# One side stream with larger loads in a hybrid attention layer: modulation and weight sums share two tiles, stores move to ScalarE's queue, biases are scaled later

## The chip, the cores and the metric

The kernel runs on one core of a Trainium2 chip. A core has a matrix engine (TensorE, PE in the profile; PEld is its loading of weights), VectorE (DVE), ScalarE (ACT), GpSimd (POOL) and SyncE (SP), which here does nothing but issue transfers. Each engine works through its own instructions in order. A transfer (DMA) is issued by an engine and then carried out by sixteen DMA engines; the issuing engine goes on. Where an instruction must wait for another engine or for a transfer, everything behind it on its engine waits as well. The metric is the device time of one execution in microseconds (us), lower is better.

## What is computed

One layer of a streaming encoder on 1024 frames of width 1024, in float32. Two attention branches of eight heads each work on the same normalised, modulated input; a gated convolutional feed-forward part follows. Cut to what matters:

```python
mod = silu(c) @ w_ada + b_ada
sh1, sc1, g1, sh2, sc2, g2 = split(mod, 6)
h = layer_norm(x) * (1 + sc1) + sh1
proj = h @ w_in          # q, k, v, forget of branch A; q, k, v of branch C; two gates
o_a = forgetting_attention(q_a, k_a, v_a, f_a + b_f)     # causal, bias from forget gates
o_c = chunk_band_attention(q_c, k_c, v_c, rel_bias)      # 64-frame chunks, 8 chunks back
merged = sigmoid(gate_a) * (o_a @ w_br_fox) + sigmoid(gate_c) * (o_c @ w_br_chunk)
x = layer_norm(alpha * x + (1 + g1) * (merged @ w_out), ln1_g, ln1_b)
h = layer_norm(x) * (1 + sc2) + sh2
a, val = split(causal_conv(h @ w_up), 2)
x = layer_norm(alpha * x + (1 + g2) * ((silu(a) * val) @ w_down), ln2_g, ln2_b)
```

## The kernel before, in words

**Products in two halves.** A float32 operand is parted into a rounded half and a remainder, and a product is made of three matmuls. For weights the rounding is a copy on ACT (L104) and the remainder a subtraction on POOL (L105, tile `wl`).

**Order of the work.** The kernel is written as one long list of operations. A planner in the compiler then gives each engine its order: it keeps to the order of the source as a priority, but an operation whose inputs and tiles are free may be taken earlier than operations of other engines that stand ahead of it in the source. A tile named with `tag` and `bufs` takes turns in that many buffers; a load into a buffer waits for the last reader of what was there.

**Attention.** Sixteen heads in eight pairs, four pairs of the chunked branch first (4, 5, 6, 7), then four of the forgetting branch (2, 3, 0, 1). For each head there are four steps of two query tiles. `scores` makes the logits on PE, adds the bias on DVE (L464) and takes the exponential on ACT (L470). `probs` turns the result on PE (L504), and ACT (L507) and DVE (L508) part it into halves in `pt`. `weighted` multiplies with the values (L518), and ACT and DVE add the two halves of the output into `o32` (L522, L523). Between the steps the loop takes units from `stream`: the projections to q, k, v and to the gates, which are the other half of PE's work in this stage. Each call of `stream.step()` yields about 2.6 us of matmuls by the source's own costs, and the loop takes as many as keep pace with attention.

**Biases.** `prep` is called for a head well before its turn. It moves the halves of the keys (L407, L408) and loads the bias. For the chunked branch that is a 128x640 table (`cb`, L414), which DVE scales at once (L415) and in which POOL fills two corners (L416, L417). For the forgetting branch it is a spread row of sums (`fb`, L411), to which POOL adds the causal mask (`fm`, L430) for each query tile.

**Stores.** A gate unit ends with a tanh on ACT (L395) into `sg`, and an output pair ends with L523. Both append their store, issued by SP, to a list `stores`, and `begun()` issues what is in the list at the next call of the stream (L295). `inverted` writes the inverse row sums through `rt` (L479, L480).

**Two side streams.** Two generators run beside, each advanced by one `yield` with every call of the stream; what is left is run behind the loop (L746).

- `late_modulation` makes the four modulation vectors that attention doesn't need. There are 64 pieces of `w_ada` (four vectors, two halves of 512 columns, eight row blocks). Each is loaded by itself (`wa`, 256 KB, two buffers, L535), multiplied by a column of `cond` on ACT (L546 for the first, L548), and added into `acc` on POOL (L549). After eight pieces PE sums `acc` over the partitions (L167), and DVE adds the bias vector (L161, L163).
- `up_sums` and `down_sums` make sums and differences of weight quarters for the feed-forward part, which multiplies by a scheme with seven products in place of eight. Nineteen times, `four` loads two weight blocks of 512 KB into one tile `dr` with a single buffer (L563), makes four sums on POOL (L568), and stores 1 MB to a scratch tensor, `wd` or `td` (L571).

Of the kernel before, what the change touches and what calls it, by code (L numbers as in the profile page):

```python
# [43 lines left out]
def body(ctx, tc, a, out):  # L44
# [337 lines left out]
    def unit_g():  # L382
        gi = next(gates)

        def run(ws):
            wh, wl = ws[0]
            for half in range(2):
# [8 lines left out]
                stores.append(partial(sy.dma_start, out=gd[half, gi], in_=sg))  # L396
# [4 lines left out]
    def prep(ip, i):  # L401
# [10 lines left out]
        else:  # L412
            b = ap.tile([P, 640], F32, name=nm("cb"), tag="bias")
            sy.dma_start(out=b, in_=a["rel_t"][h])  # L414
            ve.tensor_scalar_mul(b, b, 1.0 / SCALE)  # L415
            po.memset(b[0:DH, 576:640], NEG)  # L416
            po.memset(b[DH:P, 0:64], NEG)  # L417
        return q[i], m1, m2, b, br, h
# [6 lines left out]
    def masked(n, i):  # L425

        (ip, hi, g), qi = steps[n], 2 * steps[n][2] + i
        if ip < 4 and (n, i) not in masks:
            fm = ap.tile([P, P], F32, name=nm("fm"), tag="fm", bufs=5)
            po.tensor_tensor(out=fm, in0=heads[ip, hi][3][:, qi * P : (qi + 1) * P], in1=cmask, op=ALU.add)  # L430
            masks[n, i] = fm
# [41 lines left out]
    def inverted(ip):  # L473
# [4 lines left out]
        rt = ap.tile([n, P], F32, name=nm("rt"), tag="rt", bufs=1)  # L478
# [46 lines left out]
    def late_modulation():  # L525


        pieces = [(v, half, k) for v in (2, 4, 3, 5) for half in range(2) for k in range(KD)]
        ws = {}

        def load(n):
            if n < len(pieces):
                v, half, k = pieces[n]
                ws[n] = ap.tile([P, 1, H], F32, name=nm("wa"), tag="wa", bufs=2)
                sy.dma_start(out=ws[n], in_=ada_src(v, half * H, H)[:, k : k + 1, :])  # L535
# [5 lines left out]
        yield  # L541
        for n, (v, half, k) in enumerate(pieces):
            w = ws.pop(n)[:, 0, :]
            if k == 0:
                acc = ap.tile([P, H], F32, name=nm("acc"), tag="acc", bufs=1)
                se.mul(out=acc, in_=w, mul=cond[:, 0:1])  # L546
            else:
                se.mul(out=w, in_=w, mul=cond[:, k : k + 1])  # L548
                po.tensor_tensor(out=acc, in0=acc, in1=w, op=ALU.add)  # L549
            yield  # L550
            load(n + 2)
            if k == KD - 1:
                ps = pmm.tile([P, H], F32, name=nm("psada"), tag="mm")
                ada_sums(ps, acc, H)
                yield
                ada_bias(ps, v, half * H, H, v != 3)
            yield

    def four(steps, srcs, dst):

        x = ap.tile([P, 4, H], F32, name=nm("dr"), tag="dr", bufs=1)
        for r in range(2):
            sy.dma_start(out=x[:, 2 * r : 2 * r + 2, :], in_=srcs[r])  # L563
        yield
        yield
        yield
# [830 lines left out]
```

## Time and profile before

| | us |
|---|---|
| median of 3 runs | 1657.08 (1655.88 to 1660.12) |
| the profiled execution | 1653.7 |
| its span, first to last instruction | 1651.8 |
| PE busy | 1535.3 |
| DVE busy | 1032.1 |
| ACT busy | 789.8 |
| POOL busy | 597.1 |

The granted clock of PE is 0.970 of full speed over the span. Attention with its side streams lies at about 112 to 765 us. In a row of the timeline the numbers are the start, the duration, the engine and line, and in brackets how long the engine stood idle before it and what ended that. In a row of waits they are the total, the number of times and the longest wait. A name on the left of an arrow is written, names on the right are read; L12 is line 12 of the kernel before. SPq, ACTq and the like are an engine's queue of issues.

### The profile page before, as it was taken

How to read it: one execution, taken by the hardware profiler on the slowest of the kernel's cores; microseconds unless marked ns; L12 is line 12 of the kernel's file. 1: busy time of each engine (PE TensorE's matmuls, PEld its weight loads, DVE VectorE, ACT ScalarE, POOL GpSimd, SP SyncE). 2: the span in 40 equal slices, each digit the busy share in tenths (PEclk: the TensorE clock that was granted, in tenths of full speed). 3: DMA queues.
4: the chain of work that ended last, by engine and by line, in shares of the span. 5: the costliest groups of instructions: out<-in, count | busy, mean ns of one | idle time of the engine just before them, and what ended most of it. 6: DMA issues, size and time to landing. Idle time of an engine off the chain costs nothing. (4 is left out here: it accounts for less than half of the span.)

```text
span 1651.8 us, 22170 instructions
## 1 busy us (share of the span) xinstructions
PE 1535.3 (93%) x7693; PEld 1286.5 (78%) x7693; DVE 1032.1 (62%) x2053; ACT 789.8 (48%) x1420; POOL 597.1 (36%) x455
## 2 busy tenths in 40 slices
PE   6899889969899999998799796999999999999996
PEld 3788778859788988887677685788888888888885
DVE  6746444435444545454759978577777766856788
ACT  3447445444555555453223536444544554456451
POOL 1125536554652342223205365554455455100000
PEclk9999989979999999999999898999999999999998
DMA  9037656666643334324754624543353222597552
GB/s 363 27 103 228 206 186 209 202 207 212 213 152 99 98 122 127 109 103 150 245 180 153 237 111 158 191 140 122 129 177 135 102 96 85 198 385 239 186 196 75
DMA packets 119535, 274.82 MB, mean 166 GB/s; under 512 B 11776, under 2 KB 20672, under 8 KB 119424
## 3 DMA queue, kind: packets, MB, share of 16 engines
q1 hardware_dynamic: 114144, 264.42, 47.5%
q10 hardware_dynamic: 4752, 7.17, 1.2%
q0 software_dynamic: 528, 1.84, 0.3%
q8 instruction: 60, 0.98, 0.2%
q14 instruction: 51, 0.42, 0.1%
HBM read 197.51 MB, written 67.47 MB: 160 GB/s over the span
## 5 line engine op out<-in xcount | busy, mean ns | idle before, releaser
L105 POOL TENSOR_TENSOR wl<-ws,wh 128x1024 fp32r<-128x1024 f32 x54 | 133.4, 2474 | 263.3 <-ACT wh L104 260.6
L826 PE MATMUL psu<-hc,wx 128*128 128x512 f32 x720 | 168.4, 389 | 0.0
L826 PEld LDWEIGHTS psu<-hc,wx 128*128 128x128 f32 x720 | 135.2, 188 | 28.0
L1062 DVE SCALAR_TENSOR_TENSOR pcv<-u,convp,pcv 128x1024 f32<-128x1024 f32 x88 | 113.1, 1285 | 45.3 <-ACT pcv L1060 44.4
L568 POOL TENSOR_TENSOR dr<-dr 128x512 f32<-128x512 f32 x76 | 98.2, 1292 | 79.4 <-DMA dr<-in_w_down 48.1
L1203 DVE TENSOR_TENSOR op<-rw,op 128x512 fp32r<-128x512 f32 x146 | 93.6, 687 | 52.6 <-ACT op L1202 52.1
L1202 ACT CAST op<-rw 128x512 fp32r<-128x512 f32 x146 | 85.3, 623 | 83.4 <-PE psd L1215 39.5
L1214 PE MATMUL psd<-op,op 128*128 128x512 f32 x292 | 113.7, 389 | 0.9 <-DVE op L1203 0.9
L508 DVE TENSOR_TENSOR pt<-pst,pt 128x512 fp32r<-128x512 f32 (+1 forms) x192 | 97.1, 520 | 27.8 <-ACT pt L507 26.1
L1213 PE MATMUL psd<-op,op 128*128 128x512 f32 x292 | 113.6, 389 | 0.0
L1215 PE MATMUL psd<-op,op 128*128 128x512 f32 x292 | 113.6, 389 | 0.0
L470 ACT ACTIVATE s<-s,mx 128x640 f32<-128x640 f32 (+7 forms) x128 | 94.4, 737 | 37.9 <-DVE mx L464 35.9
L507 ACT CAST pt<-pst 128x512 fp32r<-128x512 f32 (+1 forms) x192 | 82.2, 451 | 59.9 <-PE pst L504 57.7
L207 PE MATMUL psg<-h1h,wh 128*128 128x512 f32 x256 | 105.6, 412 | 0.0
L207 PE MATMUL psq<-h1h,wh 128*128 128x512 f32 x256 | 104.4, 409 | 0.4 <-DVE h1h L203 0.4
L209 PE MATMUL psq<-h1h,wl 128*128 128x512 f32 x256 | 101.1, 395 | 2.7 <-POOL wl L105 2.7
L518 PE MATMUL pso<-pt,vs 128*128 128x256 f32 x608 | 93.8, 292 | 10.0 <-ACT pt L507 7.0
L208 PE MATMUL psq<-h1l,wh 128*128 128x512 f32 x256 | 101.4, 396 | 1.7 <-DVE h1l L204 1.7
L504 PE MATMUL pst<-ident,s 128*128 128x128 f32 x528 | 83.6, 278 | 20.5 <-DVE pt L508 20.4
L209 PE MATMUL psg<-h1h,wl 128*128 128x512 f32 x256 | 100.8, 394 | 0.0
L208 PE MATMUL psg<-h1l,wh 128*128 128x512 f32 x256 | 100.6, 393 | 0.0
L518 PEld LDWEIGHTS pso<-pt,vs 128*128 128x128 f32 x608 | 83.7, 194 | 19.4 <-ACT pt L507 11.2
(261 smaller groups left out, 3934.9 us busy)
## 6 DMA issues: line engine op xcount, KB each, us to landing
ws<-in_w_up SPq DMA_DIRECT2D x36, 512.0 KB, 3.7
wa<-in_w_ada SPq DMA_DIRECT2D x64, 256.0 KB, 3.9
dr<-in_w_down SPq DMA_DIRECT2D x22, 512.0 KB, 4.5
td<-dr SPq DMA_DIRECT2D x11, 1024.0 KB, 4.5
rw<-td SPq DMA_DIRECT2D x44, 256.0 KB, 4.5
yd<-y SPq DMA_DIRECT2D x20, 512.0 KB, 2.8
rw<-yd SPq DMA_DIRECT2D x40, 256.0 KB, 3.9
rw<-sd SPq DMA_DIRECT2D x33, 256.0 KB, 4.6
```

The source lines that it names most:

```text
L105: po.tensor_sub(out=lo, in0=st, in1=hi)
L207: pe.matmul(ps, wh, xh, start=start, stop=False)
L208: pe.matmul(ps, wh, xl, start=False, stop=False)
L209: pe.matmul(ps, wl, xh, start=False, stop=stop)
L508: ve.tensor_sub(out=dl, in0=src, in1=dh)
L518: pe.matmul(ps[:, 0:256], vs[:, h % 2, j0 + j, :], pt[j // 4][:, c, j % 4, :], start=j == 0 and c == 0, stop=j == nj - 1 and c == 1)
L568: po.tensor_tensor(out=x[:, o, :], in0=x[:, p, :], in1=x[:, q, :], op=op)
L826: pe.matmul(ps, w[:, a_, k, :], h[k][b_], start=first, stop=k == 3 and a_ == 1, skip_group_check=on)
L1062: ve.scalar_tensor_tensor(out=ps, in0=u[b][:, 2 - d : S + 2 - d], scalar=cp[:, 2 - d : 3 - d], in1=ps, op0=ALU.mult, op1=ALU.add)
L1213: pe.matmul(ps[t], g[:, 0, ts], d[:, 0], start=start, stop=False, skip_group_check=on)
L1214: pe.matmul(ps[t], g[:, 0, ts], d[:, 1], start=False, stop=False, skip_group_check=on)
L1215: pe.matmul(ps[t], g[:, 1, ts], d[:, 0], start=False, stop=stop, skip_group_check=on)
```

## The change

The two side streams become one, `side_work`. Its list of 35 groups has a weight-sum group and a modulation group by turns, and three weight-sum groups at the end. All groups use one tile `dr` of 128x4x512 with two buffers. A modulation group is four row blocks, loaded with one transfer of 1 MB; a weight-sum group has two loads of 512 KB as before. The load for group n + 2 is issued at the end of group n. Within a group two multiplies (and their adds), or two sums, stand between one `yield` and the next. The partition sums of a finished half vector stay in `ps`, and the DVE operation that adds the bias vector (`due`) is issued at the beginning of the next weight-sum group.

The stores of gate tiles are issued by ACT right behind the tanh, and those of outputs are still appended to `stores` but issued by ACT. The scaling of `cb` and the two fills leave `prep`: the tile is put on a list `unscaled`, and `scaled()` does the three operations just before the first scores of the next head. `fm` has four buffers in place of five, and `rt` takes one of them.

```diff
@@ -393,7 +393,7 @@
                         yield 2.6
                 sg = ap0.tile([P, H], F32, name=nm("sg"), tag="sg", bufs=2)
                 se.activation(out=sg, in_=ps, func=AF.Tanh, scale=0.5)
-                stores.append(partial(sy.dma_start, out=gd[half, gi], in_=sg))
+                se.dma_start(out=gd[half, gi], in_=sg)
                 yield 2.6
 
         return Unit([(a["w_g"][gi], [P, KD, P])], run, 10.4)
@@ -412,10 +412,18 @@
         else:
             b = ap.tile([P, 640], F32, name=nm("cb"), tag="bias")
             sy.dma_start(out=b, in_=a["rel_t"][h])
+            unscaled.append(b)
+        return q[i], m1, m2, b, br, h
+
+    unscaled = []
+
+    def scaled():
+
+        while unscaled:
+            b = unscaled.pop(0)
             ve.tensor_scalar_mul(b, b, 1.0 / SCALE)
             po.memset(b[0:DH, 576:640], NEG)
             po.memset(b[DH:P, 0:64], NEG)
-        return q[i], m1, m2, b, br, h
 
     def first_block(br, qi):
         return 0 if br == 0 else max(0, qi - 4)
@@ -426,7 +434,7 @@
 
         (ip, hi, g), qi = steps[n], 2 * steps[n][2] + i
         if ip < 4 and (n, i) not in masks:
-            fm = ap.tile([P, P], F32, name=nm("fm"), tag="fm", bufs=5)
+            fm = ap.tile([P, P], F32, name=nm("fm"), tag="fm", bufs=4)
             po.tensor_tensor(out=fm, in0=heads[ip, hi][3][:, qi * P : (qi + 1) * P], in1=cmask, op=ALU.add)
             masks[n, i] = fm
         return masks.get((n, i))
@@ -475,7 +483,7 @@
         n = 4 * NT
         ps = pst.tile([P, H], F32, name=nm("psr"), tag="t")
         pe.transpose(ps[0:n, 0:P], sums[:, 2 * ip * NT : 2 * ip * NT + n], ident)
-        rt = ap.tile([n, P], F32, name=nm("rt"), tag="rt", bufs=1)
+        rt = ap.tile([P, P], F32, name=nm("rt"), tag="fm", bufs=4)[0:n, :]
         ve.reciprocal(out=rt, in_=ps[0:n, 0:P])
         sy.dma_start(out=rd[2 * ip : 2 * ip + 4].rearrange("h (t s) -> (h t) s", t=NT), in_=rt)
 
@@ -522,69 +530,65 @@
         se.copy(out=tmp[own, :], in_=ps[other, 0:256])
         ve.tensor_tensor(out=o32[own, g % 2 * 256 : (g % 2 + 1) * 256], in0=ps[own, 0:256], in1=tmp[own, :], op=ALU.add)
 
-    def late_modulation():
-
-
-        pieces = [(v, half, k) for v in (2, 4, 3, 5) for half in range(2) for k in range(KD)]
-        ws = {}
+    def side_work():
+
+
+
+        sub = ALU.subtract
+        ups = ((3, 2, 3, ALU.add), (2, 0, 2, sub), (0, 3, 0, sub), (1, 1, 0, sub))
+        downs = ((0, 1, 0, sub), (1, 3, 1, sub), (3, 3, 0, sub), (2, 2, 3, sub))
+        sums_ = [(ups, a["w_up"][2 * c : 2 * c + 2].rearrange("b p (j k) n -> p b j (k n)", j=2), wd[c]) for c in range(HEAD)]
+        for i in range(NPAIR):
+            srcs = [a["w_down"][order[2 * i + r]].rearrange("p (j n) -> p j n", j=2) for r in range(2)]
+            sums_.append((downs, srcs, td[i]))
+        vecs = [(v, half, q) for v in (2, 4, 3, 5) for half in range(2) for q in range(2)]
+        groups = [g for pair in zip(sums_, vecs) for g in pair] + sums_[len(vecs) :]
+        tiles, due = {}, []
 
         def load(n):
-            if n < len(pieces):
-                v, half, k = pieces[n]
-                ws[n] = ap.tile([P, 1, H], F32, name=nm("wa"), tag="wa", bufs=2)
-                sy.dma_start(out=ws[n], in_=ada_src(v, half * H, H)[:, k : k + 1, :])
+            if n < len(groups):
+                x = tiles[n] = ap.tile([P, 4, H], F32, name=nm("dr"), tag="dr", bufs=2)
+                if n % 2 and n < 2 * len(vecs):
+                    v, half, q = groups[n]
+                    sy.dma_start(out=x, in_=ada_src(v, half * H, H)[:, 4 * q : 4 * q + 4, :])
+                else:
+                    srcs = groups[n][1]
+                    for r in range(2):
+                        sy.dma_start(out=x[:, 2 * r : 2 * r + 2, :], in_=srcs[r] if isinstance(srcs, list) else srcs[:, r])
 
         load(0)
         yield
         load(1)
         yield
-        yield
-        for n, (v, half, k) in enumerate(pieces):
-            w = ws.pop(n)[:, 0, :]
-            if k == 0:
-                acc = ap.tile([P, H], F32, name=nm("acc"), tag="acc", bufs=1)
-                se.mul(out=acc, in_=w, mul=cond[:, 0:1])
+        for n, group in enumerate(groups):
+            x = tiles.pop(n)
+            if n % 2 and n < 2 * len(vecs):
+                v, half, q = group
+                if q == 0:
+                    acc = ap.tile([P, H], F32, name=nm("acc"), tag="acc", bufs=1)
+                for j in range(4):
+                    k = 4 * q + j
+                    se.mul(out=x[:, j, :] if k else acc, in_=x[:, j, :], mul=cond[:, k : k + 1])
+                    if k:
+                        po.tensor_tensor(out=acc, in0=acc, in1=x[:, j, :], op=ALU.add)
+                    if j % 2:
+                        yield
+                if q:
+                    ps = pmm.tile([P, H], F32, name=nm("psada"), tag="mm")
+                    ada_sums(ps, acc, H)
+                    due.append(partial(ada_bias, ps, v, half * H, H, v != 3))
             else:
-                se.mul(out=w, in_=w, mul=cond[:, k : k + 1])
-                po.tensor_tensor(out=acc, in0=acc, in1=w, op=ALU.add)
+                while due:
+                    due.pop()()
+                for j, (o, p, q, op) in enumerate(group[0]):
+                    po.tensor_tensor(out=x[:, o, :], in0=x[:, p, :], in1=x[:, q, :], op=op)
+                    if j % 2:
+                        yield
+                sy.dma_start(out=group[2].rearrange("j p n -> p j n"), in_=x)
+                yield
+                yield
+            load(n + 2)
             yield
-            load(n + 2)
-            if k == KD - 1:
-                ps = pmm.tile([P, H], F32, name=nm("psada"), tag="mm")
-                ada_sums(ps, acc, H)
-                yield
-                ada_bias(ps, v, half * H, H, v != 3)
-            yield
-
-    def four(steps, srcs, dst):
-
-        x = ap.tile([P, 4, H], F32, name=nm("dr"), tag="dr", bufs=1)
-        for r in range(2):
-            sy.dma_start(out=x[:, 2 * r : 2 * r + 2, :], in_=srcs[r])
-        yield
-        yield
-        yield
-        for n, (o, p, q, op) in enumerate(steps):
-            po.tensor_tensor(out=x[:, o, :], in0=x[:, p, :], in1=x[:, q, :], op=op)
-            if n:
-                yield
-        sy.dma_start(out=dst.rearrange("j p n -> p j n"), in_=x)
-        yield
-        yield
-
-    def down_sums():
-
-        sub = ALU.subtract
-        for i in range(NPAIR):
-            srcs = [a["w_down"][order[2 * i + r]].rearrange("p (j n) -> p j n", j=2) for r in range(2)]
-            yield from four(((0, 1, 0, sub), (1, 3, 1, sub), (3, 3, 0, sub), (2, 2, 3, sub)), srcs, td[i])
-
-    def up_sums():
-
-        sub = ALU.subtract
-        for c in range(HEAD):
-            srcs = [a["w_up"][2 * c + b].rearrange("p (j k) n -> p j (k n)", j=2) for b in range(2)]
-            yield from four(((3, 2, 3, ALU.add), (2, 0, 2, sub), (0, 3, 0, sub), (1, 1, 0, sub)), srcs, wd[c])
 
 
     plan = [
@@ -693,11 +697,11 @@
         return 0.62 * pv_span(ip // 4, g)[1]
 
     ensure(0)
+    scaled()
     sts = {(0, i): scores(0, i) for i in range(2)}
     o_now = {}
     done = len(first_units)
-    beside = late_modulation()
-    aside = chain(up_sums(), down_sums())
+    beside = side_work()
     for u, (ip, _) in enumerate(plan):
         upto = done + len(groups[u])
         fill = sum(x.cost for x in groups[u])
@@ -715,6 +719,8 @@
                         while (nip not in qk or len(qk[nip]) < 2 or stream.cur <= done + 1) and nip != ip:
                             spent += stream.step()
                         ensure(n + 1)
+                    if steps[n][:2] != steps[n + 1][:2]:
+                        scaled()
                     sts[n + 1, qt] = scores(n + 1, qt)
                 probs(hd, g, qt, sts.pop((n, qt)), pt)
                 passed += 0.5 * cost_of(n)
@@ -722,12 +728,11 @@
                     spent += stream.step()
                     begun()
                     next(beside, None)
-                    next(aside, None)
             if g % 2 == 0 and i == 0:
                 o_now[ip, g // 2] = ap.tile([P, H], F32, name=nm("o32"), tag="o32", bufs=2)
             weighted(hd, g, i, pt, o_now[ip, g // 2])
             if i == 1 and g % 2 == 1:
-                stores.append(partial(sy.dma_start, out=od[g // 2, ip], in_=o_now.pop((ip, g // 2))))
+                stores.append(partial(se.dma_start, out=od[g // 2, ip], in_=o_now.pop((ip, g // 2))))
             if n + 2 < len(steps) and steps[n + 2][:2] in heads:
                 for qt in range(2):
                     masked(n + 2, qt)
@@ -743,7 +748,7 @@
         if u % 2:
             inverted(ip - 1)
     begun()
-    for _ in chain(beside, aside):
+    for _ in beside:
         pass
     ap_cm.__exit__(None, None, None)
     g1_cm, g1p = opened(name="g1", bufs=1, side="right")
```

## The prediction

> **What bounds the kernel now.** I began with the page: TensorE (PE) is busy 93% of the span, so only stretches where it is idle, or runs at a lower granted clock, can give time back. The change touches attention alone, which the trace places between 112 us (the first load of the side streams) and 765 us. The view of stages, asked for that stretch and for one of the later stages, has the columns length, then PE, PEld, DVE, ACT and POOL busy with instruction counts, then the granted clock and DMA:
>
> ```profile
> 112.00:765.00 653.00, 614.21 (x3572) 538.78 (x3572) 311.55 (x946) 342.52 (x750) 283.93 (x247) 0.97 0.51 165
> 550.00:765.00 215.00, 213.74 (x1242) 187.13 (x1243) 102.30 (x312) 106.41 (x226) 56.53 (x56) 1.00 0.35 107
> ```
>
> PE is idle 38.8 us of attention, and only 1.3 us of that lies behind 550 us. The view of waits for PE, within attention (total us, times, longest), says on whom:
>
> ```profile
> PE pst L504 <- DVE pt L508: 20.4, 4, 10.2
> PE pso L518 <- ACT pt L507: 7.0, 2, 4.4
> PE psv L310 <- POOL wl L105: 4.5, 3, 2.8
> PE pso L518 <- DVE pt L508: 2.8, 4, 1.0
> PE psq L209 <- POOL wl L105: 2.7, 2, 1.4
> ```
>
> The names are of the last link only. The timeline shows PE's gaps (in brackets), and ahead of five of them an instruction that held its engine's queue:
>
> ```profile
> 172.89 0.49 DVE L415 TENSOR_SCALAR cb<-cb 128x640 f32<-128x640 f32 x1 [8.21 <-DMA cb<-in_rel_t]
> 174.16 1.33 PE L504 MATMUL pst<-ident,s 128*128 128x128 f32 x5 [6.83 <-DVE pt L508]
> 217.15 0.72 ACT L548 ACTIVATE wa<-wa,cond 128x512 f32<-128x512 f32 x1 [8.36 <-DMA wa<-in_w_ada]
> 218.28 2.88 PE L518 MATMUL pso<-pt,vs 128*128 128x256 f32 x10 [4.39 <-ACT pt L507]
> 227.57 0.39 PE L310 MATMUL psv<-wl,h1h 128*128 128x256 f32 x1 [2.78 <-POOL wl L105]
> 336.21 0.72 ACT L548 ACTIVATE wa<-wa,cond 128x512 f32<-128x512 f32 x1 [11.03 <-DMA wa<-in_w_ada]
> 339.99 1.33 PE L504 MATMUL pst<-ident,s 128*128 128x128 f32 x5 [10.22 <-DVE pt L508]
> 359.63 0.72 ACT L548 ACTIVATE wa<-wa,cond 128x512 f32<-128x512 f32 x1 [5.70 <-DMA wa<-in_w_ada]
> 361.49 0.58 PE L518 MATMUL pso<-pt,vs 128*128 128x256 f32 x1 [2.63 <-ACT pt L507]
> 362.85 1.87 PE L518 MATMUL pso<-pt,vs 128*128 128x256 f32 x7 [0.78 <-DVE pt L508]
> 415.63 0.72 ACT L548 ACTIVATE wa<-wa,cond 128x512 f32<-128x512 f32 x1 [5.16 <-DMA wa<-in_w_ada]
> 421.23 0.77 PE L504 MATMUL pst<-ident,s 128*128 128x128 f32 x5 [2.86 <-DVE pt L508]
> ```
>
> So four of the gaps begin on ScalarE (ACT): a multiply of the modulation stream (L548) stands in its queue until its piece of `w_ada` has landed, and the copies L522 and L507 behind it keep VectorE (DVE) and then PE waiting. One begins on DVE, where the scaling of a bias (L415) waits for its load. The stages cut right behind the gaps show a second price, the clock:
>
> ```profile
> 174.10:180.00 5.90, 5.84 (x28) 5.15 (x29) 1.69 (x7) 2.47 (x6) 0.05 (x1) 0.76 0.58 206
> 218.20:224.00 5.80, 5.71 (x24) 5.32 (x25) 3.83 (x10) 4.14 (x11) 3.90 (x4) 0.50 0.02 8
> 227.50:233.00 5.50, 5.43 (x30) 5.04 (x31) 2.42 (x8) 2.14 (x6) 0.02 (x1) 0.69 1.00 276
> 340.00:344.00 4.00, 4.00 (x12) 3.42 (x13) 1.76 (x6) 2.58 (x6) 1.36 (x3) 0.50 0.88 307
> 361.40:366.00 4.60, 3.73 (x14) 3.44 (x15) 2.94 (x9) 1.90 (x5) 0.17 (x1) 0.50 0.60 226
> 421.00:425.00 4.00, 3.77 (x24) 3.77 (x25) 0.94 (x6) 0.87 (x2) 1.27 (x1) 0.71 0.99 347
> ```
>
> Busy time times one minus the clock is what the slow clock cost: 1.4, 2.9, 1.7, 2.0, 1.9 and 1.1 us.
>
> **The pot, in three terms.** A, modulation: gaps 4.39 + 10.22 + 2.63 + 0.78 + 2.86 = 20.9, clock 2.9 + 2.0 + 1.9 + 1.1 = 7.9, together 28.8 us. B, bias: 6.83 + 1.4 = 8.2 us. C, weight halves that GpSimd (POOL) delivers late: 4.5 + 2.7 of waits and 1.7 of clock = 8.9 us. In all 45.9 us, and no more can come from attention.
>
> The clock term can be weighed against the Trainium skill ("TensorE: Matmul & The Clock Gate", Part 1: The HAM clock gate): TensorE drops to half clock after an idle window of about 3.4 us. The 0.50 behind the gaps of 4.39 and 10.22 us agrees; the 0.50 and 0.71 behind gaps of 2.63 and 2.86 us do not follow from it. By the rule the pot would be 3.0 us smaller; I go by the rows.
>
> **The change, part by part.** These are the prices of its operations, from the grouped waits, the lists of DMA issues (count, KB each, median us to landing) and the single lines:
>
> ```profile
> ACT wa L548 <- DMA wa<-in_w_ada: 69.0, 31, 11.0
> POOL dr L568 <- DMA dr<-in_w_down: 48.1, 9, 9.7
> POOL cb L416 <- DVE cb L415: 28.9, 7, 12.6
> SPq L295 <- ACT sg L395: 107.6, 22, 10.6
> wa<-in_w_ada SPq DMA_DIRECT2D x64, 256.0 KB, 3.9
> wa<-in_w_ada SPq DMA_DIRECT2D x8, 1024.0 KB, 11.0
> td<-dr SPq DMA_DIRECT2D x11, 1024.0 KB, 4.5
> L571 SPq DMA_DIRECT2D td<-dr x11: 377/377/427, 282.8 to 458.8; - x11
> L535 SPq DMA_DIRECT2D wa<-in_w_ada x64: 327/328/1113, 113.2 to 615.3; - x64
> L856 ACTq DMA_DIRECT2D md<-mc x16: 326/326/378, 984.8 to 1051.6; - x16
> ```
>
> *One stream instead of two.* The 64 multiplies, 56 accumulating adds and 76 sums stay, on the same engines; 64 loads of 256 KB become 16 of 1 MB, so 48 issues of 0.33 us leave SP, which costs PE nothing either way. What changes is when a load starts. Now a modulation piece is asked for one piece ahead, two yields. Then a group is asked for when the tile of the group two before is free, with a whole weight-sum group (five yields) between. An in-order reading would cover any landing time of the rows above, and A would go wholly. But the trace shows that the queues do not follow the source: counted from its costs, the loop makes 164 calls, the weight sums need 152 of them, and yet the last `td` store goes out at 458.8 us and not near 700. The compiler's planner pulls side work forward as far as its tiles are free. The modulation stream is held back by its accumulator, which PE must have read (its last load is at 615.3). In the new stream each half vector has two groups: the first waits for the accumulator and finds its data landed, the second can follow as soon as its tile is reloaded, so its first multiply may still stand on ACT until the load lands. That is 8 tight groups, against 64 pieces. I price one at the mean wait now, 69.0 / 31 = 2.2 us, and turn ACT waiting into lost time at the rate of now, 28.8 / 69.0 = 0.42: 8 x 2.2 x 0.42 = 7.4 us stay, so A gives 21.4 us. Ends: 28.8 with every wait covered; a loss with long landings, which is the third rival.
>
> *Bursts.* Two multiplies and two adds stand together per yield. Four multiplies in a row are four times 0.72, 2.9 us, which ACT's other work waits behind; the 5.16 us wait above cost PE 2.86, so the burst costs nothing or little as long as it stays single. I take zero, with the end at 0.42 x 16 x 2.9 = 19 us if PE always waited.
>
> *Weight sums.* Their adds wait less for loads (48.1 us of POOL waiting for `in_w_down` now), but the shared two tiles tie their pace to the modulation groups, so they spread over some 112 to 650 us instead of 112 to 460. POOL is thinner where PE waits for it and fuller behind. For C I take nothing, ends -8.9 to +8.9 us.
>
> *Late scaling.* The scaling and the two fills move in the source from the load to just before the head's first scores. If the queues follow, DVE meets a landed bias, and the 28.9 us of POOL waiting in the fills go too: B gives 8.2. If the planner pulls it forward again, B gives nothing. I take half, 4.1, as no row decides it.
>
> *Stores on ACT.* 32 gate and 16 output stores leave SP's queue, where they held it 107.6 us behind the tanh, mostly behind 500 us where PE hardly waits; what stood behind them was loads. On ACT each takes an issue of 0.33 us: 48 x 0.33 = 16 us of an engine busy 342.5 of 653 us, between instructions that PE awaits. A gate store waits for the tanh just ahead of it, an output store for DVE's add; queued behind are the copies L507 and exponentials L470. Ends 0 and 16 x 0.42 = 7 us lost. I take zero, since an ACT wait over ten times as long (5.16 us) cost PE 2.86 us.
>
> *Small tiles.* `fm` falls from five to four buffers and `rt` joins them.
>
> ```profile
> POOL fm L430 <- DVE mx L464: 97.5, 32, 7.7
> ```
>
> POOL already waits 97.5 us for DVE before `fm`, and PE, which is hardly idle behind 550 us, does not show it; zero, and at worst a part of C's 8.9.
>
> *Sum.* 21.4 + 4.1 = 25.5 us. The profiled execution took 1653.7 us, 1.9 above its span of 1651.8, so 1628.2 by it. The median of the three runs shown, 1657.08, lies 3.4 us above that execution; 1657.1 - 25.5 gives **1632 us**. Later stages only start earlier.
>
> **The rivals.** *All waits go*: 45.9 us, so 1611. For it: one load ahead by a group is longer than any landing above, and behind 550 us PE shows that this mix can run without gaps. Against: the planner's pulling forward.
>
> *The waits only move.* The planner places each multiply by its own idea of a landing, and ACT then waits 69 us as before, in fewer and longer pieces; only B's half goes, 1657.1 - 4.1 = 1653, which counts as no change, because a measurement of this kernel tells about 0.3% (5 us) from none. For it: 31 of 64 pieces waited though each was asked for a piece ahead. Against: the longest waits came with a queue of small loads behind POOL. Of the stores on the second queue the Trainium skill ("DMA: Bandwidth & Descriptors", Issuing engines are not separate DMA queues) says that all queues run on the same DMA engines and only the sequencer's issue time is saved; by that alone this rival would hold, and the 107.6 us that SP stood behind the tanh are what it leaves out.
>
> *Slower: the long load.* A 1 MB load holds up the whole group. It landed in 11.0 us in the crowded start, against 4.5 for stores of that size. If the 8 tight groups each wait as ACT did ahead of 218 us (8.36), each costs 4.39 + 2.9 = 7.3 us, 58 in all against the 37.0 of A and B: +21, so 1678. It decides from 37.0 / 8 = 4.6 us lost per tight group. For it: strict order on ACT makes one late load stop everything. Against: DMA engines are half busy (0.51) in attention.
>
> **How the numbers follow.** Chances: the forecast 0.51 (its own range 1618 to 1646), all waits gone 0.15, only moved 0.16, long load 0.18. Faster 0.51 + 0.15 = 0.66, same 0.16, slower 0.18. The range from 1608 to 1662 takes in the first three with the ends of the unknown costs and leaves the slow rival out.
>
> **What would show it.** Right: the row of ACT's modulation multiply waiting for its DMA falls to about 18 us; PE idle in attention falls from 38.8 to some 15 us with clock 0.99; DVE no longer waits for `rel_t`; weight sums run on past 600 us. Wrong: multiplies that wait 5 us or more for a 1 MB load; PE gaps that end on POOL's `wl`, behind longer runs of adds; the scaling still placed at its landing; new gaps behind 550 us, where there were none.

## The result, and the profile after

The kernel with the change took 1680.12 us (median of 4 runs, 1672.64 to 1686.70) against 1657.09 us (median of 4, 1655.88 to 1660.12) before: a ratio of 1.0135, 95% interval 1.0088 to 1.0181. It is 23 us, or 1.35%, slower. The forecast was 1632, with a range up to 1662. The profiled execution of after took 1677.85 us, its span 1675.7. Of the nine runs of p_stores, a kernel of the experiments below, one took 2887.05 us at a granted clock of 0.863 and the others 1664.70 to 1674.97 us; its ratio leaves that one out.

**Where the time went.** The last value product of attention (`pso`) is a good mark of the stage's end. These two views of before are the list of instructions of that tile (duration min/median/max in ns, first and last start in us) and the windows behind the mark and in the first 588 us of attention:

```profile
L518 PE MATMUL pso<-pt,vs x608: 276/283/582, 123.2 to 752.8; 128*128 128x256 f32 x152
...
752.80:1651.80 899.00, 842.97 (x3688) 689.60 (x3686) 657.94 (x921) 406.31 (x601) 299.29 (x197) 0.97 0.49 169
112.00:700.00 588.00, 549.21 (x3221) 482.94 (x3221) 282.47 (x869) 311.65 (x690) 272.53 (x239) 0.97 0.54 172
```

The same two views of after:

```profile
L526 PE MATMUL pso<-pt,vs x608: 276/283/583, 122.9 to 774.6; 128*128 128x256 f32 x152
...
774.60:1675.70 901.10, 845.56 (x3688) 692.18 (x3686) 653.12 (x921) 405.99 (x601) 297.41 (x197) 0.97 0.49 169
112.00:700.00 588.00, 534.45 (x3107) 468.81 (x3107) 273.66 (x829) 299.26 (x667) 266.12 (x231) 0.95 0.52 170
```

The mark lies 21.8 us later, and the rest of the span is 2.1 us longer with the same 3688 matmuls. So the loss is in attention. In its first 588 us PE is idle 53.6 us in place of 38.8, and its clock is 0.95 in place of 0.97; it got through 3107 matmuls in place of 3221.

**What PE waited for.** The waits of after: PE's first (112 to 800 us), then those of ACT and DVE (112 to 765 us) and of SP's queue (112 to 700 us) that bear on the change (total us, times, longest):

```profile
PE pso L526 <- ACT pt L515: 11.6, 4, 5.6
PE pst L512 <- DVE pt L516: 9.7, 3, 5.6
PE psv L309 <- ACT wh L104: 8.1, 1, 8.1
PE pss L460 <- DVE mx L472: 5.6, 4, 3.1
PE psq L209 <- POOL wl L105: 4.3, 1, 4.3
...
ACT dr L571 <- DMA dr<-in_w_ada: 41.8, 8, 9.5
ACT dr L571 <- issue: 23.4, 4, 10.9
DVE cb L424 <- DMA cb<-in_rel_t: 22.0, 5, 7.3
SPq L553 <- POOL acc L573: 28.3, 7, 8.9
SPq L553 <- DMA td<-dr: 17.2, 4, 5.1
SPq L553 <- DMA wd<-dr: 7.8, 2, 3.9
```

ACT still stands before the multiply of the modulation (now L571): 41.8 us put down to its load and 23.4 us to "issue", which is a wait whose cause the profile doesn't name. That makes 65.2 us against 69.0 before, but in 12 waits and not in 31: 5.4 us each in place of 2.2. DVE still stands before the scaling of the bias, 22.0 us against 17.8 before.

The timeline of after shows how these waits reach PE. Each line gives start, duration and the instruction, and in brackets the idle time ahead of it:

```profile
186.06 1.95 ACT L571 ACTIVATE dr<-dr,cond 128x512 f32<-128x512 f32 x3 [6.33 <-DMA dr<-in_w_ada]
188.32 0.58 PE L526 MATMUL pso<-pt,vs 128*128 128x256 f32 x1 [5.59 <-ACT pt L515]
...
229.53 0.72 ACT L571 ACTIVATE dr<-dr,cond 128x512 f32<-128x512 f32 x1 [5.56 <-DMA dr<-in_w_ada]
230.73 0.58 PE L526 MATMUL pso<-pt,vs 128*128 128x256 f32 x1 [5.39 <-ACT pt L515]
...
339.91 0.49 DVE L424 TENSOR_SCALAR cb<-cb 128x640 f32<-128x640 f32 x1 [6.99 <-DMA cb<-in_rel_t]
341.18 1.33 PE L512 MATMUL pst<-ident,s 128*128 128x128 f32 x5 [5.62 <-DVE pt L516]
343.14 1.33 ACT L571 ACTIVATE dr<-dr,cond 128x512 f32<-128x512 f32 x2 [9.51 <-DMA dr<-in_w_ada]
...
548.72 0.38 SPq L587 DMA_DIRECT2D td<-dr  x1
554.73 0.38 SPq L553 DMA_DIRECT2D dr<-in_w_ada  x1
560.07 1.33 ACT L571 ACTIVATE dr<-dr,cond 128x512 f32<-128x512 f32 x2 [10.87 <-issue]
565.06 0.58 PE L309 MATMUL psv<-wh,h1h 128*128 128x256 f32 x1 [8.13 <-ACT wh L104]
...
592.54 9.51 POOL L573 TENSOR_TENSOR acc<-acc,dr 128x512 f32<-128x512 f32 x7 [2.53 <-ACT acc L571]
606.03 0.80 PE L209 MATMUL psg<-h1h,wl 128*128 128x512 f32 x1 [3.99 <-POOL wl L105]
```

The first two pairs are the gap of before in its pure form: a multiply at the head of ACT's queue, and PE idle almost as long. At 340 us the bias and the multiply stand at the same time on two engines. The pair at 560 us shows the wait without a name. The load was issued at 554.73, 6.0 us behind a store of weight sums, and the multiply began 5.3 us after that issue. ACT had stood since 549.2. Roughly half of its wait lies before the load was even asked for. The rows of SP's queue (L553 issues the 16 loads of the modulation) say why: 6 of them wait for a store of weight sums (`td` or `wd`) to have landed, 7 for POOL's adds. At 592 us seven adds run in one piece of 9.5 us, with the weight halves behind them.

The clock behind three of these gaps and behind a smaller one, as windows of after:

```profile
230.70:236.00 5.30, 5.27 (x24) 5.27 (x25) 2.66 (x9) 4.18 (x9) 0.00 (x0) 0.50 0.34 76
565.00:571.00 6.00, 5.57 (x26) 5.28 (x27) 0.29 (x1) 1.62 (x5) 2.37 (x1) 0.54 0.31 96
606.00:610.00 4.00, 3.96 (x9) 3.15 (x10) 0.00 (x0) 0.00 (x0) 2.30 (x1) 0.50 0.53 167
176.20:180.00 3.80, 3.74 (x21) 3.26 (x22) 2.25 (x8) 3.12 (x9) 3.64 (x4) 1.00 0.23 91
```

Behind the gaps of 5.39, 8.13 and 3.99 us PE ran at about half clock. The last window lies behind a gap of 2.99 us and shows full clock, while before had 0.50 behind one of 2.63 us. So the length of the gap alone doesn't decide it near 3 us. The Trainium skill ("TensorE: Matmul & The Clock Gate", Part 1: The HAM clock gate) calls the window in which activity is counted free-running. Two short gaps with different outcomes agree with that; no run here shows the window itself.

### The profile page after: what moved, and what is told of

Same layout as the page of the kernel before. It is cut to its first block, busy times and chain, and to the rows that moved or that the text cites. A ratio compares the mean times of both kernels' runs of the same rounds, so it can differ in the third digit from the quotient of the medians.

```text
span 1675.7 us, 22014 instructions
## 1 busy us (share of the span) xinstructions
PE 1544.7 (92%) x7693; PEld 1293.0 (77%) x7693; DVE 1029.6 (61%) x2053; ACT 788.1 (47%) x1420; POOL 594.4 (35%) x455
## 5 line engine op out<-in xcount | busy, mean ns | idle before, releaser
L515 ACT CAST pt<-pst 128x512 fp32r<-128x512 f32 (+1 forms) x192 | 82.5, 450 | 56.4 <-PE pst L512 54.6
```

## The experiments

In all of them the times are medians of the runs of that kernel, and each ratio is to the kernel before, measured beside it on the same chip (1655.75 to 1657.35 us), with its 95% interval. "Mark" is the start of the last value product. The expectations were on record before each kernel ran.

| kernel | us | ratio | mark |
|---|---|---|---|
| before | 1657.09 | 1 | 752.8 |
| after | 1680.12 | 1.0135 [1.0088, 1.0181] | 774.6 |
| p_stores | 1667.53 | 1.0063 [1.0042, 1.0084] | 762.3 |
| p_scaled | 1656.12 | 0.9994 [0.9977, 1.0011] | 752.7 |
| p_stream | 1672.20 | 1.0081 [1.0059, 1.0104] | 768.5 |
| a_pinned | 1650.06 | 0.9960 [0.9942, 0.9977] | 745.7 |
| b_pinned | 1660.45 | 1.0019 [1.0006, 1.0033] | 759.2 |
| a_pinned2 | 1647.28 | 0.9944 [0.9923, 0.9966] | 747.4 |
| a_pinned2_sp | 1645.00 | 0.9932 [0.9911, 0.9952] | 741.4 |
| a_pieces | 1683.04 | 1.0160 [1.0143, 1.0177] | 780.0 |
| a_pinned3 | 1637.25 | 0.9887 [0.9869, 0.9904] | 732.1 |
| a_pinned3_sp | 1629.27 | 0.9843 [0.9818, 0.9868] | 731.1 |
| a_pinned4 | 1603.36 | 0.9680 [0.9664, 0.9697] | 698.2 |
| a_pinned4_sp | 1603.55 | 0.9671 [0.9651, 0.9691] | 697.6 |
| b_pinned4 | 1604.64 | 0.9686 [0.9664, 0.9708] | 703.6 |

The question was whether the loss comes from what the change transfers (one long load in place of four short ones), from who issues what, or from the places that the planner gives the side work in each engine's order.

### One part at a time

**p_stores**: before, with the 48 gate and output stores issued by ACT and nothing else.

```diff
-                stores.append(partial(sy.dma_start, out=gd[half, gi], in_=sg))
+                se.dma_start(out=gd[half, gi], in_=sg)
...
-                stores.append(partial(sy.dma_start, out=od[g // 2, ip], in_=o_now.pop((ip, g // 2))))
+                stores.append(partial(se.dma_start, out=od[g // 2, ip], in_=o_now.pop((ip, g // 2))))
```

> The kernel before with the gate and output stores on ScalarE's queue and nothing else of the change. Theory (the loss comes from 1 MB modulation loads for which ScalarE stands): no change, 1652 to 1662 us, since the 48 issues of 0.33 us are spread over 650 us. Rival 1 (the issues on ScalarE delay the copies that TensorE waits for): 1662 to 1675 us. Rival 2 (any small edit makes the planner write another order, and orders differ by 10 us and more whatever the edit): a move of over 8 us either way.

It cost 10 us, where the theory said nothing; the ranges of both rivals hold it. Two rows of its waits, and ahead of them the bias row of before:

```profile
DVE cb L415 <- DMA cb<-in_rel_t: 17.8, 5, 8.2
...
PE pst L504 <- DVE pt L508: 34.7, 6, 8.8
DVE cb L415 <- DMA cb<-in_rel_t: 29.6, 6, 7.9
```

PE's wait behind DVE grew from 20.4 to 34.7 us, and DVE's wait for the bias table from 17.8 to 29.6 us. In the timeline four gaps of PE now follow a scaling that stood for its table (6.52, 6.17, 2.79 and 2.94 us), where before had one (6.83). The stores have nothing to do with the bias table, except that they stood on the queue that loads it. So a change in one place moved waits in another. This run alone can't say whether another small edit would have done the same by chance.

**p_scaled**: before, with only the late scaling (`unscaled`, `scaled()` and its two calls, as in the change).

> The kernel before with the late scaling of the biases and nothing else. Theory: no change, 1652 to 1662 us, and VectorE still waits about 18 us for the bias tables, since the planner puts the scaling where it expects the table to have landed, wherever the source has it. Rival 1 (the late place is kept in the order): VectorE's wait for the tables goes to under 3 us and the time falls to about 1649 us. Rival 2 (orders differ by chance): a move of over 8 us either way.

No difference that can be told: 1.2 us, inside the interval. DVE's wait for the tables is smaller than the 17.8 us of before, but it is still there:

```profile
DVE cb L424 <- DMA cb<-in_rel_t: 11.3, 4, 4.8
```

The scaling now stands in the source just before the head's first scores, long behind its load, and on DVE it still waits for that load. The fourth table is asked for at 163.94 us and scaled at 169.75; before it was 167.12 and 172.89, the same 5.8 us. So the engine's order doesn't follow the move.

**p_stream**: before, with only the single stream and the four shared `fm` buffers. Against after it reads:

```diff
-                se.dma_start(out=gd[half, gi], in_=sg)
+                stores.append(partial(sy.dma_start, out=gd[half, gi], in_=sg))
...
-            unscaled.append(b)
...
-        while unscaled:
-            b = unscaled.pop(0)
...
-    scaled()
...
-                stores.append(partial(se.dma_start, out=od[g // 2, ip], in_=o_now.pop((ip, g // 2))))
+                stores.append(partial(sy.dma_start, out=od[g // 2, ip], in_=o_now.pop((ip, g // 2))))
```

> The kernel before with the single side stream and the four small buffers alone; stores on SyncE and early scaling as before. Theory (the stream makes the loss): 1672 to 1686 us, near the changed kernel, with ScalarE standing 55 us or more in all for the modulation groups, in some ten waits of 3 to 11 us. Rival 1 (the stores make the loss): within 5 us of 1657. Rival 2 (chance of orders): anything, and then the waits of ScalarE for the groups differ much from those of the changed kernel.

It cost 14.9 us, as the theory said. ACT's waits and the window of attention:

```profile
ACT dr L563 <- issue: 27.9, 5, 12.2
ACT dr L563 <- DMA dr<-in_w_ada: 26.9, 7, 5.8
...
112.00:700.00 588.00, 538.73 (x3132) 472.46 (x3131) 274.10 (x835) 302.32 (x673) 269.30 (x233) 0.95 0.51 170
```

Twelve waits again, now 54.8 us, less than the 69.0 of before, and yet PE is idle 49.3 us and the clock is 0.95. Not all of that begins on ACT: DVE waits 27.9 us for the bias tables here. The three parts by themselves make 10.2 - 1.2 + 14.9 = 23.9 us, and the change 23.0.

### Is it the length of the transfer?

**a_pieces**: after, with each load of 1 MB issued as four of 256 KB into the same tile.

```diff
-                    sy.dma_start(out=x, in_=ada_src(v, half * H, H)[:, 4 * q : 4 * q + 4, :])
+                    for j in range(4):
+                        sy.dma_start(out=x[:, j : j + 1, :], in_=ada_src(v, half * H, H)[:, 4 * q + j : 4 * q + j + 1, :])
```

> The changed kernel with each 1 MB load of a modulation group issued as four loads of 256 KB into the same tile; nothing held. Theory (the waits come from where the multiply is placed and from when SyncE gets to issue the load; the length of the transfer is a small part): ScalarE's waits for the groups stay above 45 us and the time within 8 us of 1680. Rival (the long transfer is what is waited for, since a 256 KB piece lands in 3.9 us and a 1 MB group in 5.4): waits fall below 35 us and the time to 1665 or less.

1683.04 us, no gain. The lists of DMA issues (KB each, median us to landing) of after, and then of this kernel:

```profile
dr<-in_w_ada SPq DMA_DIRECT2D x16, 1024.0 KB, 5.4
```

```profile
dr<-in_w_ada SPq DMA_DIRECT2D x64, 256.0 KB, 4.2
```

A long load lands only 1.2 us later than a short one, and ACT still stands 59.0 us for its pieces (50.2 put down to the loads, 8.8 to issue). So cutting the load up gives nothing, and a_pinned, next, keeps the loads of 1 MB and loses ACT's waits. The length is not the cause.

### Is it the place in the engine's order?

**a_pinned**: after, with each multiply held on ACT behind the exponential that stands before it in the source. `issue_after` tells the planner not to place what stands in it ahead of the named instruction. Both are on one engine, and nothing else is changed.

```diff
-        se.activation(out=st[:, 0:nk], in_=st[:, 0:nk], func=AF.Exp, scale=-1.0, bias=prev, accum_out=sums[:, col : col + 1])
+        last[0] = se.activation(out=st[:, 0:nk], in_=st[:, 0:nk], func=AF.Exp, scale=-1.0, bias=prev, accum_out=sums[:, col : col + 1])
...
-                    se.mul(out=x[:, j, :] if k else acc, in_=x[:, j, :], mul=cond[:, k : k + 1])
+                    with tc.issue_after(last[0].ins):
+                        se.mul(out=x[:, j, :] if k else acc, in_=x[:, j, :], mul=cond[:, k : k + 1])
```

> The changed kernel with one thing more: each modulation multiply may not be placed on ScalarE ahead of the exponential that stands before it in the source, so that the planner can't pull it forward to its own estimate of the landing. Theory (pulled-forward multiplies standing for late loads cost the time): ScalarE's waits for the modulation groups fall from 65 us to under 15 us, the TensorE gaps that begin there go, and the time falls by 20 us or more, to 1660 or below; if the first forecast's pot is right as well, below 1645. Rival 1 (the loads are late at the source's own place too, because the two tiles come free late): waits stay above 40 us and the time above 1670. Rival 2 (the loss lies with GpSimd's sums or the stores): waits fall and the time stays above 1670.

30 us less than after, and 7 less than before; the theory said 1660 or below. In ACT's waits there is no row of the multiply any more. New in PE's waits and timeline:

```profile
PE psada L167 <- POOL acc L575: 20.7, 2, 12.0
...
174.12 1.87 PE L167 MATMUL psada<-ones,acc 128*128 128x1 f32 x8 [8.75 <-POOL acc L575]
```

PE itself now stands: the planner has placed the partition sums of `acc` ahead of PE's other work, and POOL's adds come up to 12.0 us later.

**b_pinned**: before, with its own multiplies (L546, L548) held in the same way.

> The kernel before (two streams, 256 KB pieces) with its modulation multiplies held behind the exponential that stands before them in the source. Theory (the multiplies stand on ScalarE because they are pulled forward, with small and with large loads): ScalarE's waits for the pieces fall from 69 us to under 20 us, and the time falls by 10 to 28 us to 1629 to 1647 us, unless TensorE then stands for the partition sums, as it does in the changed kernel with held multiplies (two gaps, 20.7 us). Rival (small pieces are asked for only two yields ahead, so they come late at the source's place too): waits above 40 us and no change in time.

1660.45 us, no gain over before. The waits of the multiply fell from 69.0 to 10.6 us, as the theory had it, but its 10 to 28 us of gain didn't come. PE stands for the partition sums, the exception that it had named, and other rows took over as well (DVE's wait for the bias tables is 26.6 us):

```profile
PE psada L167 <- POOL acc L552: 13.3, 1, 13.3
PE psv L310 <- POOL wl L105: 13.0, 3, 8.7
```

So holding one kind of side work moves the stand to the next kind.

**a_pinned2** and **a_pinned2_sp**: a_pinned, with the partition sums issued behind the four sums of the next weight-sum group and held on PE behind the last score matmul; the second has the stores back on SP.

```diff
+                if due:
+                    done_acc, v, half = due.pop()
+                    ps = pmm.tile([P, H], F32, name=nm("psada"), tag="mm")
+                    with tc.issue_after(last[1].ins):
+                        ada_sums(ps, done_acc, H)
+                    ada_bias(ps, v, half * H, H, v != 3)
```

> The changed kernel with held multiplies, and with the partition sums of a half vector moved behind the next weight-sum group and held behind the score matmuls that stand before them in the source. Theory: TensorE's two gaps of 8.75 and 11.98 us before the partition sums were the same fault on another engine (an operation placed by the planner's estimate, ahead of late adds); they go, and the time falls by 15 to 25 us from 1650 to about 1625 to 1635. Rival 1 (the gaps move to the next late thing): 1645 to 1655. Rival 2 (the held sums keep the accumulator too long, and the stream falls behind): the weight sums end behind 750 us and the time rises above 1655.

> The same with the gate and output stores back on SyncE's queue. Theory A (the stores alone cost 10 us on the kernel before only because the planner wrote another order, with other waits for loads): within 5 us of the run with the stores on ScalarE. Theory B (the issues on ScalarE cost time by themselves): 6 to 12 us faster than that run. Theory C (on SyncE the stores hold up the loads behind them): 4 us slower or more.

A miss for the theory, and the range of the rival by which the gaps move on: 1647.28 and 1645.00, hardly better than a_pinned. The timeline of a_pinned2 shows what stands now:

```profile
183.61 0.49 DVE L424 TENSOR_SCALAR cb<-cb 128x640 f32<-128x640 f32 x1 [15.05 <-DMA cb<-in_rel_t]
185.12 0.69 PE L461 MATMUL pss<-qm,qm 128*128 128x384 f32 x1 [10.02 <-DVE mx L473]
```

**a_pinned3** and **a_pinned3_sp**: a_pinned2, with the late scaling held on DVE behind the last bias addition; the second again with the stores on SP.

```diff
-            ve.tensor_scalar_mul(b, b, 1.0 / SCALE)
+            with tc.issue_after(last[2].ins) if last[2] else ExitStack():
+                ve.tensor_scalar_mul(b, b, 1.0 / SCALE)
```

> The changed kernel with held multiplies and partition sums, and with the late scaling of the biases held on VectorE behind the bias additions that stand before it in the source. Theory: now the late place is kept, VectorE's wait for the tables falls from about 9 us to under 2 us, and the time falls by 0 to 8 us against the run without this. Rival (the held scaling comes too late and delays the first scores of a head): slower by 3 us or more, with VectorE or TensorE gaps at the changes of head.

> The changed kernel with held multiplies, partition sums and scalings, and with the stores back on SyncE. Theory (stores on ScalarE cost nothing by themselves): within 4 us of 1637. Rival (each issue on ScalarE delays it): 1631 or less.

1637.25 and 1629.27 us; the first is 2 us better than was expected, and for the second it was the rival that had 1631 or less. DVE's wait for the bias table is gone: the fourth table is asked for at 175.94 us and scaled at 199.95. What is left, in the timeline of a_pinned3, begins on POOL:

```profile
512.42 5.35 POOL L583 TENSOR_TENSOR dr<-dr 128x512 f32<-128x512 f32 x4 [3.28 <-DMA dr<-in_w_down]
517.73 2.34 POOL L105 TENSOR_TENSOR wl<-ws,wh 128x1024 fp32r<-128x1024 f32 x1
520.12 0.58 PE L310 MATMUL psv<-wl,h1h 128*128 128x256 f32 x1 [5.12 <-POOL wl L105]
```

POOL waits for a load, makes four sums, and only then the weight half for which PE is idle.

**a_pinned4** and **a_pinned4_sp**: a_pinned3, with the weight sums held on POOL behind the last weight half or mask.

```diff
-        po.tensor_sub(out=lo, in0=st, in1=hi)
+        wl_last[0] = po.tensor_sub(out=lo, in0=st, in1=hi)
...
-                    po.tensor_tensor(out=x[:, o, :], in0=x[:, p, :], in1=x[:, q, :], op=op)
+                    with tc.issue_after(wl_last[0].ins):
+                        po.tensor_tensor(out=x[:, o, :], in0=x[:, p, :], in1=x[:, q, :], op=op)
```

> The changed kernel with held multiplies, partition sums and scalings, and GpSimd's weight sums held behind the weight halves and masks that stand before them in the source. Theory (the gaps left, 12.5 us behind late weight halves, come from sums that stand on GpSimd for their loads ahead of the halves): those gaps shrink and the time falls by 3 to 12 us from 1637. Rival (the halves come after the sums in the source too, so that holding them changes little): within 3 us of 1637, with the same gaps.

> The changed kernel with all four kinds held (multiplies, partition sums, scalings, weight sums) and the stores back on SyncE. If the stores cost by themselves (48 issues that delay ScalarE's copies): 4 to 10 us faster than 1603, to 1599 or less. If their cost in the other pairs came from where waits fell in the planner's order: within 3 us of 1603, since attention has only 1.5 us of TensorE gaps left to give.

1603.36 us, 34 less than a_pinned3, where 3 to 12 were expected. That went by the 12.5 us of gaps whose last link was a weight half; PE was idle 23.8 us in the window of a_pinned3, and its clock was 0.97. The mark and the window of a_pinned4:

```profile
L530 PE MATMUL pso<-pt,vs x608: 276/283/394, 121.1 to 698.2; 128*128 128x256 f32 x152
...
112.00:700.00 588.00, 586.53 (x3523) 519.18 (x3522) 312.02 (x939) 336.17 (x744) 284.62 (x247) 1.00 0.55 180
```

PE is idle 1.5 us in 588, at full clock. The mark lies 54.6 us earlier than before. The stores back on SP give 1603.55, which is the same: who issues them is worth nothing once the order is kept.

**b_pinned4**: before, with its two streams, its 256 KB pieces and its stores on SP, the late scaling, and the same four kinds held (the partition sums two yields later).

> The kernel before, with its two streams and stores on SyncE, with late scaling, and with the same four kinds held. Theory A (placement is all): within 6 us of the changed kernel with all held, 1597 to 1610. Theory B (the larger loads asked for a group ahead are worth something once the places are kept): 1612 to 1645, with ScalarE or GpSimd still waiting for pieces that are asked for two yields ahead and with one buffer for the weight sums.

1604.64 us, 1.3 above a_pinned4 and within both intervals, as theory A said. Its window, and two rows of its waits:

```profile
112.00:700.00 588.00, 582.83 (x3490) 515.11 (x3489) 311.51 (x936) 335.80 (x741) 281.42 (x246) 1.00 0.57 179
...
ACT wa L562 <- DMA wa<-in_w_ada: 6.2, 3, 4.1
POOL dr L585 <- DMA dr<-in_w_down: 39.6, 10, 7.4
```

POOL still waits 39.6 us for loads of weight sums, but PE is idle only 5.2 us. So one stream of larger transfers gives nothing to the whole time that the places don't give. In attention alone it may give some 5 us: the mark of b_pinned4 lies 5.4 us later than that of a_pinned4, and what follows is 6.9 us shorter (897.3 against 904.2 us, one profile each).

The rival that any edit gives another order, and another time by chance, was on record for p_stores. p_scaled's 1.2 us and the three kernels that meet at 1603 to 1605 us with the places held, whatever their stores and streams, speak against it for the whole; for the 10 us of p_stores it stays open.

On size the Trainium skill ("DMA: Bandwidth & Descriptors", Bandwidth) says to batch transfers to 1 MiB or more for most of the peak rate. That holds for a rate; here the DMA engines are about half busy (0.57), and 256 KB or 1 MB made no difference to the time, with the places free (1683.04 and 1680.12) or held (1604.64 and 1603.36).

## Why the prediction was wrong

**Right in the main: the pot and where it lies.** Idle time and clock in attention were put at 45.9 us, and no more was said to be there; a_pinned4 brings the mark forward by 54.6 us. PE's idle time in the first 588 us falls from 38.8 to 1.5, so 37.3 us of it is idle time (34.9 in the pot). The other 17.3 us is time for which PE was busy: 602.0 us from 112 us to the mark before, 584.7 in a_pinned4, for the same matmuls. About 12 of it is the clock: busy time times one minus the clock, summed over windows of 4 us, makes 11.9 us before and nothing in a_pinned4, so the 11.0 us of the clock in the pot were well read. Where the other 5 us come from is open. The 3.0 us by which a rule on idle windows would make the pot smaller count the gaps of 2.63 and 2.86 us; the 1.7 us behind 2.78 us belong with them, which makes 4.7.

**Wrong: term A, the modulation.** This is the step that failed: "8 tight groups" at 2.2 us of waiting each, 17.6 us in all, so that 21.4 of 28.8 us would be saved. Measured were 12 waits with 65.2 us. Two readings in it were wrong. The load was taken to be asked for a group ahead, but it can only be issued when its buffer is free, and the timeline at 548 to 560 us shows a store of weight sums that had to land first. And the mean wait of a 256 KB piece, 2.2 us, was taken for a group, which waits 5.4 us. With 65.2 us at its own rate of 0.42, 27.4 us would have stayed: A would have given 1.4 us, no gain, but no loss either. The step that turned ACT's waiting into lost time at a constant 0.42 fails with it: p_stream has 14 us less waiting than before (54.8 against 69.0) and is 14.9 us slower. Of the 31 waits before, four are followed by the gaps of term A; a wait above 5 us can pass to PE nearly whole (6.33 gave 5.59, 10.87 gave 8.13) and takes the clock along. What decides is the place of the multiply: held behind its exponential (a_pinned), with the same loads, it doesn't wait at all, and 30 us go. The part with term A cost 14.9 us in place of saving 21.4: 36.3 us of the 48.5 by which the forecast was off. A part of that begins on DVE, where the waits for the bias tables grew to 27.9 us; it was not parted from the rest.

**Wrong in size: the stores.** Taken as 0, with 7 at the most; alone they cost 10.2. The mechanism weighed there, 48 issues between ACT's instructions, is worth nothing, as a_pinned4 and its twin show (1603.36 and 1603.55). What p_stores shows in its place are longer waits for the bias tables, with three gaps of PE more; that they come from a new order is argued from this, and no row of before shows them.

**Wrong in size: term B, the bias.** Taken as 4.1 us, half of 8.2; alone it gave 1.2, which can't be told from nothing. "If the planner pulls it forward again, B gives nothing" was the case that came: 22.0 us of DVE waiting for the bias table in after, 17.8 before. Held in its place, as in a_pinned3, the same edit was worth 10 us (1647.28 to 1637.25), with other waits moved too.

**Right: no loss behind attention, and weight sums that spread.** The list of the tile's instructions in after has the last store of weight sums, which went out at 458.8 us before:

```profile
L587 SPq DMA_DIRECT2D td<-dr x11: 377/377/383, 336.7 to 638.0; - x11
```

It goes out at 638.0 us, and the rest of the span changes by 2.1. The sign that was given as wrong for C, weight halves late behind longer runs of adds, is there at 592 to 606 us. The other three signs of being wrong came too: waits of 5 us and more for a load of 1 MB, the scaling placed at its landing, and new gaps behind 550 us (8.13 and 3.99).

**The rivals.** The slow rival foretold 1678, close to the 1680.12, and its place (a multiply at the head of ACT's queue) is right. Its mechanism is not: a load of 1 MB lands in 5.4 us, and four short loads in its stead changed nothing. Its sum, 8 groups at 7.3 us, meets the total by chance, since the stream alone makes 15 of the 23 us. "The waits only move" had the mechanism that the runs bear out best, a planner that places each multiply by its own idea of a landing, and also said that ACT would wait as long in fewer and longer pieces (65.2 against 69.0 us); it priced them as if longer pieces cost the same. The range, too, was narrower than was said: 1632 with its own ends for bursts (19), stores (7) and C (8.9) is 1667, above its upper end of 1662.

**What stays open.** By which rule the planner places an operation was not tried; that it reckons with earlier landings than the trace shows is argued from the waits, and what the runs show is that the places decide. The stores on SP were 2 and 8 us better in a_pinned2 and a_pinned3 and not in a_pinned4; which waits made that was not taken apart. Nor was the gain of a_pinned4's last edit alone, which came on top of the three others, nor the 5 us of PE's busy time that the clock doesn't explain.

## What to carry to other kernels

Engines work in order, so before pricing an edit that moves or enlarges a load, look where the instruction that needs it stands in its engine's queue, and what PE needs from behind it: a few long stands cost more than many short ones of the same total. Where a planner orders the work, a later place in the source is not a later place on the engine; hold side work behind an instruction of its own engine, and all kinds of it, since holding one only brings the next to the fore (1650, 1647, 1637, then 1603 us). And try the parts of a change singly: an edit that is worth nothing with the order held (1603.36 and 1603.55) cost 10 us without.

## What was unexpected of the hardware

The gain came with the places of four kinds of small operations on four engines: with all held, PE ran 586.53 of 588 us at a granted clock of 1.00, where before had 549.21 us at 0.97. The clock is thus a good part of what a gap costs: about 12 of the 54.6 us by the windows of 4 us. Behind gaps near 3 us it went either way, 1.00 after 2.99 us and 0.50 after 2.63 us.
